# A new order of the work slots in the token mixers of a one-layer hybrid decoder

## The chip, the cores and the metric
The kernel runs on one core of one Trainium2 chip. The metric is the device time of one execution in microseconds, as the median over runs of the same program.

## What is computed
One layer of a decoder runs for a prompt of 256 tokens and for 8 sample tokens with the same weights, all in float32, so 264 columns stand side by side. The layer has token mixers, cross-attention into 256 memory tokens, and a squared-ReLU MLP. The change touches the token mixers alone:

```python
proj = x @ p["w_in"] + p["b_in"]      # columns for four branches and four gates per channel
# A gated DeltaNet: short conv on q, k, v, then the chunked delta rule, 8 heads, gated RMSNorm
out_a = rms_norm(o_a, p["a_norm_w"]) * silu(z_a)
# B Conformer convolution: GLU, depthwise conv of width 31, LayerNorm, swish
u_b, _ = causal_dwconv(a_b * sigmoid(g_b), conv_b, p["b_conv_w"])
out_b = silu(layer_norm(u_b + p["b_conv_b"], p["b_ln_g"], p["b_ln_b"]))
# C short gated convolution, width 3
out_c = bg_c * causal_dwconv(cg_c * h_c, conv_c, p["c_conv_w"])[0]
# D mLSTM matrix memory, 4 heads
y = sum_n(sigmoid(gate_n) * (branch_n @ w_branch_n)) @ p["w_out"]
```

The chunked rules of A and D also update states, which are outputs too.

## The kernel before
**Slots.** All large matrix products are cut into 704 slots. A slot is one weight tile of 128 x 1024 floats: 24 matmuls of 264 columns, since every product is made of three (high x high, high x low, low x high parts of both operands). *slot* (line 207) appends a weight source, a function for TensorE and, at the end of an output block, a *post* function that takes the block out of PSUM. *gin* (line 371) makes one output block of the input projection, two slots. *run* (line 289) walks through the slots. In each it issues the load of a later weight tile, its conversion to the high part on ScalarE (*feed*, line 266) and the split into the low part (*feed_lo*, line 278) two slots ahead. Every fourth split goes to GpSimd, the others to VectorE (line 209).

**Work between the slots.** Two queues of Python generators hold the rest. *chain* has the serial work: the row stage (line 480), the four delta rule units (*a_unit*, line 688, two heads each), the norm of branch B (*b_norm*, line 988) and the two mLSTM units (*d_unit*, line 1071). In each slot *run* issues at most one step of the generator at its head, and then steps of *fill* as long as a planned VectorE time is not ahead of a planned TensorE time:

```python
            if chain and dv_t[0] < lim:
                step(chain)
            while fill and dv_t[0] < lim:
                step(fill)
```

The plan counts 2.72 us a slot (line 303) and a formula for VectorE (line 116). *drain* (line 223) steps a queue until a given generator is through. The instructions are then scheduled once more, by priority in the order of issue (line 1840). TensorE, VectorE, ScalarE, GpSimd and SP each run their queue in order.

**Branch A.** *a_gemm(u)* (line 1264) makes the six blocks of q, k, v for unit u. Each one's post function (*a_block*, line 622) does a convolution of width 4 on VectorE and a sigmoid on ScalarE. The last one appends the unit to *chain*. *a_begin* (line 613) runs at the first block of units 2 and 3 and drains the unit two before it, whose buffer it takes. A unit has a front (norms of q and k: matmuls ssl2q, ssl2k; products KQ and G; masks), five levels of a triangular inverse (matmuls xb, ub, tb), and four chunks (matmuls ks, db, ob, sb) with the states of the sample tokens (DMA dbc, tile s) between them.

**Branch B.** *b_block(j)* (line 955), called a gated block here, makes one of eight blocks: four slots, a gate by exp, ln, exp on ScalarE (*sigmoid*, line 166), and then *b_conv* (line 936), 30 VectorE instructions (tile cB) that go to *fill*. *b_block(j)* drains the convolution two before it. *b_norm* normalises all eight blocks.

**Branch C.** *c_block(j)* (line 897) makes one of eight blocks in six slots, with some six VectorE instructions. The result goes to pairC.

**Output stages.** *phase2(n, pair, first)* (line 1003) makes, for each of 16 output blocks, the gate (two slots, the hardware's sigmoid function on ScalarE) and the branch's product (one slot). The first one is for branch C, in slots 128 to 175.

**The order.** Units 0 and 1 of branch A are first, then B and C blocks in turn, with units 2 and 3 between:

```python
    a_gemm(0)
    a_gemm(1)
    bc((0, 1))
    a_gemm(2)
    bc((2, 3, 4))
    a_gemm(3)
    bc((5, 6, 7))
    phase2(2, "C", True)
```

Of the kernel before, what the change touches and what calls it, by code (L numbers as in the profile page):

```python
# [26 lines left out]
NB = BW // P  # L27
# [64 lines left out]
def decoder_step(ctx, tc, A, O):  # L92
# [12 lines left out]
    def X16(name, dt=F32R):  # L105
        return xp.tile([P, KB, NT], dt, tag="x16", name=name)
# [15 lines left out]
    def act(out, in_, func, bias=0.0, scale=1.0, **kw):  # L122
        return AC.activation(out, in_, func, bias=bias, scale=scale, **kw)  # L123

    def tt(out, a, b, op, eng=None):
        if eng is None:
            cost(out)
        return (eng or DV).tensor_tensor(out=out, in0=a, in1=b, op=op)  # L128

    def ts(out, a, s1, op0, s2=None, op1=None):  # L130
        cost(out, 0.6)
        if op1 is None:
            DV.tensor_scalar(out, a, s1, None, op0=op0)
        else:
            DV.tensor_scalar(out, a, s1, s2, op0=op0, op1=op1)

    def stt(out, a, s, b, op0, op1):
        cost(out, 1.1)
        return DV.scalar_tensor_tensor(out=out, in0=a, scalar=s, in1=b, op0=op0, op1=op1)  # L139
# [14 lines left out]
    def split(hi, lo, src):  # L154
        act(hi, src, AF.Copy)
        tt(lo, src, hi.bitcast(F32), SUB)
# [9 lines left out]
    def sigmoid(g, src, bias=None):  # L166
        if bias is None:
            ts(g, src, -80.0, MAX)
        else:
            ts(g, src, bias, ADD, -80.0, MAX)  # L170
        act(g, g, AF.Exp, scale=-1.0)
        act(g, g, AF.Ln, bias=ones[:, 0:1])
        act(g, g, AF.Exp, scale=-1.0)
# [17 lines left out]
    def col(name, i=0, n=1):  # L191
        o, w = _pc[name]
        return pc[:, o + i:o + i + n]
# [8 lines left out]
    chain, fill = deque(), deque()  # L202
# [12 lines left out]
    def step(q):  # L215
        try:
            next(q[0])
            return True
        except StopIteration:
            q.popleft()  # L220
            return False

    def drain(g):
        for q in (chain, fill):
            while g in q:
                step(q)
# [12 lines left out]
    def later(n, f):  # L239
        todo.append((now[0] + n, f))  # L240

    def store(dst, src):
        later(DELAY, lambda: dma(dst, src))
# [127 lines left out]
    def gin(start, post):  # L371
        i = BI[start]
        gemm(A["win"][i - 1], xs, 2, lambda ps: post(ps, col("bin", i)))
# [221 lines left out]
    def sconv(win, wc, W, dst, eng=None):  # L595
        t = tp.tile([P, NS, W], F32, tag="cw%d" % W, name="cw", bufs=1)
        tt(t[:], win, wc[:, None, :].to_broadcast([P, NS, W]), MUL, eng=GP)
        DV.reduce_sum(out=dst, in_=t[:], axis=AX.X)
        cost(t[:])
# [292 lines left out]
    def newpair(name):  # L892
        return xp.tile([P, 2, NB, NT], F32R, tag="x16", name=name)
# [3 lines left out]
    def c_block(j):  # L897
        st = {}

        def post_h(ps, bc):  # L900
            if j == 0:
                drain(rowg[0])
                pr["C"] = newpair("pairC")
            st["h"] = tp.tile([P, NT], F32, tag="ht", name="ht", bufs=1)
            act(st["h"][:], ps, AF.Identity, bias=bc)

        def post_c(ps, bc):
            e = tp.tile([P, 30 + NT], F32, tag="ext", name="extC", bufs=1)
            GP.memset(e[:, 0:2], 0.0)
            stt(e[:, 2:2 + NT], ps, bc, st["h"][:], ADD, MUL)  # L910
            GP.tensor_copy(winC[:, j, :, 2], e[:, 2 + NP:2 + NT])
            GP.tensor_copy(scp[:, j, :], e[:, NP:NP + 2])
            wc = col("cC", 3 * j, 3)
            v = tp.tile([P, NT], F32, tag="cu", name="cuC", bufs=1)
            act(v[:, 0:NP], e[:, 0:NP], AF.Copy, scale=wc[:, 0:1])
            for i in range(1, 3):
                stt(v[:, 0:NP], e[:, i:i + NP], wc[:, i:i + 1], v[:, 0:NP], MUL, ADD)
            sconv(winC[:, j], wc, 3, v[:, NP:])
            st["v"] = v

        def post_b(ps, bc):
            v = st["v"]
            stt(v[:], ps, bc, v[:], ADD, MUL)
            split(pr["C"][:, 0, j, :], pr["C"][:, 1, j, :], v[:])
            if j == NB - 1:
                store(O["sc_p"], scp[:])
                store(O["sc_s"], winC[:])

        gin(O_H + P * j, post_h)
        gin(O_CG + P * j, post_c)  # L930
        gin(O_BG + P * j, post_b)

    bst = {}
    bgen = {}

    def b_conv(j, e):
        cB = bst["cB"]
        wc = col("cB", 31 * j, 31)
        dst = cB[:, j, :]
        act(dst[:, 0:NP], e[:, 0:NP], AF.Identity, bias=col("bcb", j), scale=wc[:, 0:1])  # L940
        yield
        for i in range(1, 31):
            stt(dst[:, 0:NP], e[:, i:i + NP], wc[:, i:i + 1], dst[:, 0:NP], MUL, ADD)
            if i % 2 == 0:
                yield
        if j == 0:
            bst["m"] = mean0(cB, w1)
        tt(dst, dst, bst["m"][:], SUB, eng=GP)
        bst["ln"].add(j)

    def win_b(j):
        bst["w"] = tp.tile([P, NS, 31], F32, tag="winB", name="winB", bufs=2)
        dma(bst["w"][:], A["sB"][:, j])

    def b_block(j):
        st = {}

        def post_a(ps, bc):
            if j == 0:
                bst["cB"] = w1.tile([P, NB, NT], F32, tag="h8", name="cB", bufs=2)  # L960
                bst["ln"] = Norm(bst["cB"], NB, "B", w1, True)
            st["a"] = tp.tile([P, NT], F32, tag="ht", name="at", bufs=1)
            act(st["a"][:], ps, AF.Identity, bias=bc)

        def post_g(ps, bc):
            if j >= 2:
                drain(bgen[j - 2])
            g = tp.tile([P, NT], F32, tag="sg", name="gB")
            sigmoid(g[:], ps, bc)
            e = tp.tile([P, 30 + NT], F32, tag="extB", name="extB")  # L970
            win = bst["w"]
            if j < NB - 1:
                later(3, lambda: win_b(j + 1))
            GP.memset(e[:, 0:30], 0.0)
            tt(e[:, 30:], st["a"][:], g[:], MUL, eng=GP)
            GP.tensor_copy(win[:, :, 30], e[:, 30 + NP:])
            store(O["gl_p"][:, j], e[:, NP:NP + 30])
            store(O["gl_s"][:, j], win[:])
            dst = bst["cB"][:, j, NP:]
            sconv(win, col("cB", 31 * j, 31), 31, dst)  # L980
            ts(dst, dst, col("bcb", j), ADD)
            bgen[j] = b_conv(j, e)
            fill.append(bgen[j])

        gin(O_GLU + P * j, post_a)
        gin(O_GLU + BW + P * j, post_g)

    def b_norm():
        for j in range(NB):
            drain(bgen[j])  # L990
        ln = bst["ln"]
        yield from ln.finish()
        yield
        for j in range(NB):
            t = ln.block(j, col("blg", j), pool=j % 2)
            sg = tp.tile([P, NT], F32, tag="ht", name="sgB", bufs=1)
            act(sg[:], t, AF.Sigmoid, bias=col("blb", j))
            stt(t, t, col("blb", j), sg[:], ADD, MUL)
            yield

    merged = []

    def phase2(n, pair, first):
        for d in range(KB):
            st = {}

            def post_g(ps, bc, d=d, st=st):
                if first and d == 0:
                    merged.append(X16("merged", F32))
                st["s"] = tp.tile([P, NT], F32, tag="sg", name="gate")  # L1010
                last["SIG"] = act(st["s"][:], ps, AF.Sigmoid, bias=bc)

            def post_p(ps, d=d, st=st):
                sg = st["s"]
                m = merged[0][:, d, :]
                if first:
                    tt(m, ps, sg[:], MUL)
                else:
                    tt(sg[:], ps, sg[:], MUL)
                    tt(m, m, sg[:], ADD, eng=GP)  # L1020
                if n == 3:
                    split(mhl[0][:, d, :], mhl[1][:, d, :], m)

            gin(O_G + D * n + P * d, post_g)
            gemm([A["wbr"][n, d]], lambda: (pr[pair][:, 0], pr[pair][:, 1]), 1, post_p)
# [239 lines left out]
        for i in range(4 if u == 0 else 0, 6):  # L1265
            gin(O_QKV + P * ((i // 2) * 8 + 2 * u + i % 2), a_block(u, i))

    def bc(js):
        for j in js:
            b_block(j)  # L1270
            c_block(j)

    a_gemm(0)
    a_gemm(1)
    bc((0, 1))
    a_gemm(2)
    bc((2, 3, 4))
    a_gemm(3)
    bc((5, 6, 7))
    phase2(2, "C", True)  # L1280
    bng = b_norm()
    mark(lambda: chain.append(bng))
    mark(lambda: [drain(agen[u]) for u in range(4)])
# [569 lines left out]
```

## Time and profile before
| | us |
|---|---|
| median of 3 runs | 2326.68 |
| lowest and highest run | 2324.32, 2328.25 |
| the profiled execution | 2324.7 |
| its span | 2322.9 |
| TensorE busy in the span | 2249.0 (97%) |
| VectorE busy | 1269.8 (55%) |
| ScalarE busy | 1167.0 (50%) |
| GpSimd busy | 977.8 (42%) |

Times in the profile count from the start of the span. PE is TensorE, DVE is VectorE, ACT is ScalarE, POOL is GpSimd, PEld are TensorE's weight loads. Busy shares are over the whole span and mix stages with different limits. A matmul is named by the tile that it writes and the tiles that it reads: g<-xh,wl is one of the 24 of a slot.

### The profile page before, as it was taken

The numbers are of one execution on the slowest core, as the hardware profiler recorded it, in microseconds if no ns is written. First come the engines' busy times: TensorE is split into PE (matmuls) and PEld (weight loads), VectorE is DVE, ScalarE is ACT, GpSimd is POOL, SyncE is SP. The second block draws the span as 40 slices with busy tenths as digits, with TensorE's granted clock in tenths as the row PEclk, the third lists the DMA queues.
The fourth block names the chain that finished last, engine by engine and source line by source line (L and its number), as shares of the span: only waits on it lengthen the run. The fifth ranks groups of instructions, "written<-read, shape, count | busy, mean of one in ns | idle before, by whom it ended". The sixth has DMA issues, their size and how long they took to land.

```text
span 2322.9 us, 46442 instructions
## 1 busy us (share of the span) xinstructions
PE 2249.0 (97%) x19034; PEld 2205.4 (95%) x19034; DVE 1269.8 (55%) x2039; ACT 1167.0 (50%) x1789; POOL 977.8 (42%) x733
## 2 busy tenths in 40 slices
PE   9899999989999999999989999989999999999997
PEld 8899898989999999999989998889999999999997
DVE  7998998894464455433474566385323323323323
ACT  6756456554554455544434555456435435534543
POOL 4535335341222133433243365165445544544576
PEclk9999999999999999999999999999999999999998
DMA  7556455554656676765556666545565565566553
GB/s 233 166 151 201 137 174 167 169 165 143 193 173 185 195 221 215 211 182 182 182 183 182 200 200 201 187 132 181 181 182 176 179 182 181 174 183 181 176 180 127
DMA packets 125134, 418.81 MB, mean 180 GB/s; under 512 B 15608, under 2 KB 20984, under 8 KB 124920
## 3 DMA queue, kind: packets, MB, share of 16 engines
q1 hardware_dynamic: 124920, 415.84, 58.4%
q8 instruction: 149, 2.44, 0.4%
q14 instruction: 65, 0.53, 0.1%
HBM read 401.37 MB, written 14.41 MB: 179 GB/s over the span
## 4 chain that ended last, share of the span: by engine, by line
PE 81%; DVE 13%; issue 3%; DMA 1%; ACT 1%; POOL 1%; DVEq 0%; POOLq 0%; ACTq 0%; SPq 0%
PE g L150 73%; DVE cB L139 3%; DVE wl L128 3%; PE q L150 1%; DVE cu L139 1%; DVE y L128 1%; PE pv L150 1%; DVE y L139 1%; DMA dbc<-dd 1%; PE ub L150 0%; PE xb L150 0%; DVE s L139 0%; PE cb L150 0%; ACT wh L123 0%; PE nb L150 0%
## 5 line engine op out<-in xcount | busy, mean ns | idle before, releaser
L123 ACT ACTIVATE wh<-raw 128x1024 fp32r<-128x1024 f32 (+1 forms) x705 | 745.4, 1058 | 822.4 <-PE g L150 306.3
L128 POOL TENSOR_TENSOR wl<-raw,wh 128x1024 fp32r<-128x1024 f32 x240 | 588.0, 2450 | 724.7 <-PE g L150 483.2
L150 PE MATMUL g<-xh,wl 128*128 128x264 f32 x2496 | 714.0, 286 | 8.1 <-DVE wl L128 6.0
L150 PE MATMUL g<-xl,wh 128*128 128x264 f32 x2496 | 717.2, 287 | 0.0
L150 PE MATMUL g<-xh,wh 128*128 128x264 f32 x2496 | 716.1, 287 | 0.9 <-ACT wh L123 0.9
L128 DVE TENSOR_TENSOR wl<-raw,wh 128x1024 fp32r<-128x1024 f32 (+1 forms) x465 | 589.8, 1269 | 231.2 <-PE g L150 169.6
L150 PEld LDWEIGHTS g<-xh,wl 128*128 128x128 f32 x2496 | 473.0, 190 | 10.2 <-DVE wl L128 6.6
L150 PEld LDWEIGHTS g<-xh,wh 128*128 128x128 f32 x2496 | 473.5, 190 | 5.3 <-issue 2.5
L150 PEld LDWEIGHTS g<-xl,wh 128*128 128x128 f32 x2496 | 472.2, 189 | 2.3 <-issue 1.3
L150 PE MATMUL g<-hgh,wl 128*128 128x264 f32 x1024 | 290.4, 284 | 0.0
L150 PE MATMUL g<-hgl,wh 128*128 128x264 f32 x1024 | 290.4, 284 | 0.0
L150 PE MATMUL g<-hgh,wh 128*128 128x264 f32 x1024 | 289.9, 284 | 0.0
L150 PE MATMUL g<-zh,wh 128*128 128x266 f32 x960 | 275.1, 287 | 0.8 <-DVE zw L128 0.8
L150 PE MATMUL g<-zl,wh 128*128 128x266 f32 x960 | 274.6, 286 | 0.0
L150 PE MATMUL g<-zh,wl 128*128 128x266 f32 x960 | 274.4, 286 | 0.0
L150 PEld LDWEIGHTS g<-hgl,wh 128*128 128x128 f32 x1024 | 193.0, 188 | 0.0
L150 PEld LDWEIGHTS g<-hgh,wh 128*128 128x128 f32 x1024 | 192.5, 188 | 0.0
L150 PEld LDWEIGHTS g<-hgh,wl 128*128 128x128 f32 x1024 | 192.4, 188 | 0.0
L128 DVE TENSOR_TENSOR y<-y,g 128x264 f32<-128x264 f32 x80 | 34.3, 429 | 278.7 <-PE g L150 278.7
L150 PEld LDWEIGHTS g<-zh,wh 128*128 128x128 f32 x960 | 181.4, 189 | 1.0 <-ACT wh L123 1.0
L150 PEld LDWEIGHTS g<-zl,wh 128*128 128x128 f32 x960 | 181.7, 189 | 0.0
L150 PEld LDWEIGHTS g<-zh,wl 128*128 128x128 f32 x960 | 180.8, 188 | 0.0
(481 smaller groups left out, 3449.3 us busy)
## 6 DMA issues: line engine op xcount, KB each, us to landing
raw<-in_win_dram SPq DMA_DIRECT2D x312, 512.0 KB, 4.0
raw<-in_f_dram SPq DMA_DIRECT2D x248, 512.0 KB, 4.2
raw<-in_wbr_dram SPq DMA_DIRECT2D x64, 512.0 KB, 4.0
raw<-in_wout_dram SPq DMA_DIRECT2D x32, 512.0 KB, 4.3
s<-in_sS_dram SPq DMA_DIRECT2D x8, 512.0 KB, 5.0
dbc<-dd SPq DMA_DIRECT2D x16, 256.0 KB, 3.7
out_S_s_dram<-s SPq DMA_DIRECT2D x8, 512.0 KB, 5.2
c<-in_sCm_dram SPq DMA_DIRECT2D x8, 512.0 KB, 5.7
```

The costliest lines, as they stand in the source:

```text
L123: return AC.activation(out, in_, func, bias=bias, scale=scale, **kw)
L128: return (eng or DV).tensor_tensor(out=out, in0=a, in1=b, op=op)
L139: return DV.scalar_tensor_tensor(out=out, in0=a, scalar=s, in1=b, op0=op0, op1=op1)
L150: PE.matmul(out, lhsT, rhs, start=start, stop=stop)
```

## The change
The blocks of branch C come ahead of most of branch B. Only four gated blocks are left before the output stage of branch C. The other four stand inside it, ahead of its output blocks 1, 5, 9 and 12. The projections of units 2 and 3 start 12 and 8 slots later. *b_norm* no longer drains the convolutions: it yields until all eight blocks are made and none is left in *fill*.

```diff
     def b_norm():
-        for j in range(NB):
-            drain(bgen[j])
+        while len(bgen) < NB or any(g in fill for g in bgen.values()):
+            yield
         ln = bst["ln"]
...
-    def phase2(n, pair, first):
+    def phase2(n, pair, first, between={}):
         for d in range(KB):
+            if d in between:
+                b_block(between[d])
             st = {}
...
-    def bc(js):
-        for j in js:
-            b_block(j)
-            c_block(j)
-
     a_gemm(0)
     a_gemm(1)
-    bc((0, 1))
+    c_block(0)
+    b_block(0)
+    c_block(1)
+    c_block(2)
+    c_block(3)
+    b_block(1)
     a_gemm(2)
-    bc((2, 3, 4))
+    c_block(4)
+    b_block(2)
+    c_block(5)
+    c_block(6)
+    b_block(3)
     a_gemm(3)
-    bc((5, 6, 7))
-    phase2(2, "C", True)
+    c_block(7)
+    phase2(2, "C", True, {1: 4, 5: 5, 9: 6, 12: 7})
```

## Rows read from the trace of the kernel before

**Rows 1.** The page's slices: busy tenths of TensorE and VectorE in 40 equal parts

```profile
PE   9899999989999999999989999989999999999997
...
DVE  7998998894464455433474566385323323323323
```

**Rows 2.** The chain that ended last: start us, us, what; a stretch without waits

```profile
972.04 195.07 PE g L150 x1608
```

**Rows 3.** Windows A:B, length; busy us of PE, PEld, DVE, ACT, POOL; clock; DMA

```profile
119.00:187.00 68.00, 65.26 (x659) 63.12 (x654) 63.14 (x122) 32.11 (x58) 17.95 (x22) 1.00 0.50 148
...
240.00:352.00 112.00, 105.33 (x1026) 101.90 (x1026) 107.19 (x198) 50.58 (x88) 38.91 (x43) 0.98 0.53 158
352.00:399.00 47.00, 42.11 (x387) 40.36 (x385) 37.95 (x58) 32.91 (x61) 28.35 (x41) 1.00 0.55 173
399.00:477.00 78.00, 78.00 (x780) 76.19 (x777) 68.99 (x136) 37.68 (x70) 23.48 (x26) 1.00 0.54 166
477.00:516.00 39.00, 32.42 (x251) 30.95 (x250) 37.33 (x58) 23.91 (x35) 18.31 (x14) 0.96 0.53 164
```

**Rows 4.** Windows, as in rows 3: before the output stage, and the output stage

```profile
93.00:516.00 423.00, 399.74 (x3761) 387.11 (x3761) 379.17 (x667) 232.50 (x414) 175.20 (x206) 0.99 0.55 168
516.00:665.00 149.00, 148.20 (x1394) 145.75 (x1394) 67.81 (x107) 69.76 (x102) 30.08 (x17) 1.00 0.56 169
```

**Rows 5.** Waits of TensorE from 93 to 516 us: total us, times, longest

```profile
PE KQ L150 <- DVE qkv L128: 5.3, 2, 3.0
PE ssl2q L150 <- ACT sql2q L123: 4.4, 2, 2.6
PE xb L150 <- DVE m_u L128: 3.1, 2, 1.8
PE ks L150 <- DVE S L139: 2.9, 2, 2.0
PE xb L150 <- DVE m_u L818: 2.8, 3, 1.9
PE db L150 <- DVE vt L139: 2.1, 2, 1.2
```

**Rows 6.** Windows, as in rows 3: two stretches at a low clock

```profile
288.00:291.40 3.40, 3.40 (x17) 3.40 (x17) 3.22 (x10) 3.22 (x9) 0.16 (x1) 0.52 0.00 0
...
513.20:516.60 3.40, 3.40 (x17) 3.40 (x17) 3.40 (x8) 0.18 (x1) 1.03 (x2) 0.51 0.75 258
```

**Rows 7.** VectorE's groups from 93 to 516 us: busy us, mean ns, idle before

```profile
L139 DVE SCALAR_TENSOR_TENSOR cB<-extB,pc,cB 128x256 f32<-128x256 f32 x239 | 145.7, 610 | 8.1 <-ACT cB L123 4.3
L128 DVE TENSOR_TENSOR wl<-raw,wh 128x1024 fp32r<-128x1024 f32 x82 | 107.1, 1307 | 5.9 <-PE g L150 3.6 <-issue 2.0 <-ACT wh L123 0.3
```

**Rows 8.** Tile merged: ns min/median/max, first and last start us

```profile
L128 DVE TENSOR_TENSOR merged<-g,gate x16: 418/433/435, 511.8 to 665.0; 128x264 f32<-128x264 f32 x16
```

**Rows 9.** Windows, as in rows 3: projections of the third and fourth unit

```profile
179.00:222.00 43.00, 40.05 (x327) 39.39 (x326) 34.86 (x66) 25.73 (x48) 21.29 (x35) 1.00 0.66 210
344.00:385.00 41.00, 36.11 (x293) 34.83 (x292) 36.14 (x51) 29.05 (x55) 26.23 (x39) 1.00 0.54 170
```

**Rows 10.** Timeline of ScalarE from 609 us: start us, us, instruction

```profile
609.82 0.46 ACT L123 ACTIVATE gate<-g,pc 128x264 f32<-128x264 f32 x1
610.30 1.28 ACT L123 ACT_TABLE_LOAD   x1
...
612.47 1.28 ACT L123 ACT_TABLE_LOAD   x1
...
614.31 2.11 ACT L123 ACTIVATE wh<-raw 128x1024 fp32r<-128x1024 f32 x2
```

**Rows 11.** Tiles winB, sgB and KQd, columns as in rows 8

```profile
L237 SPq DMA_DIRECT2D winB<-in_sB_dram x8: 425/426/1551, 22.1 to 442.9; - x8
...
L123 ACT ACTIVATE sgB<-cB,pc x8: 499/514/517, 675.2 to 691.4; 128x264 f32<-128x264 f32 x8
...
L150 PE MATMUL KQd<-qkvD x32: 222/222/270, 759.1 to 867.6; 128*64 128x64 f32 x32
```

## The prediction
> **What bounds the kernel now.** I read the page's slices first. TensorE is full in nearly every slice. VectorE is nearly full in the first nine (up to about 520 us) and between 30% and 60% for most of the rest [rows 1]. So the stage that the change reorders has two engines close to their limit, and the rest has one. Where TensorE has nothing to wait for, a slot of 24 matmuls costs 24 x 195.07 / 1608 = 2.91 us [rows 2]. The change neither adds nor removes a matmul, so it can only win or lose time in which TensorE stands, or runs at half clock.
>
> That time I read from stretches of the span [rows 3]. 119 to 187 and 240 to 352 us are long stretches with gated-block convolutions nearly without a break. VectorE is 93% and 96% busy there, and TensorE stands 68 - 65.26 = 2.7 us and 112 - 105.33 = 6.7 us. 352 to 399 us has the end of the fourth unit's projections and the front of the third unit's delta rule, no convolution, VectorE at 81%: TensorE still stands 4.9 us. 399 to 477 us has VectorE at 88% and TensorE loses nothing. 477 to 516 us holds the last convolutions and the front of the fourth unit: VectorE 96%, 6.6 us lost. Over 93 to 516 us that is 423 - 399.74 = 23.3 us, and 516 to 665 us (the output stage of the short convolution) adds 0.8 us [rows 4].
>
> So VectorE's share alone doesn't say where time goes: 88% costs nothing, 93 to 96% does, and a unit's front costs at 81% as well. The waits say why [rows 5]: TensorE takes its queue in order, and a small matmul of the delta rule stands at its head until a result comes from VectorE (KQ, xb, ks) or ScalarE (ssl2q). Two of the longer waits are followed by 3.4 us with about half the clock granted, 1.2 GHz instead of 2.4: 17 matmuls in 3.4 us [rows 6]. At full clock 17 take 17 x 0.1213 = 2.06 us, so each costs 1.3 us, 2.7 us together. What can be won at most is 23.3 + 0.8 + 2.7 = 26.8 us.
>
> **The change, part by part.**
>
> *Four gated blocks go to the output stage.* One block brings 30 convolution steps of 0.610 us mean, 18.3 us of VectorE, four slots, three of whose splits fall to VectorE at 1.31 us [rows 7], and three small steps, put at the 0.43 us of a pass over one output block [rows 8], 1.3 us. The stretch 93 to 516 us has 379 us of VectorE in 423 us, 90% [rows 4]. It loses 4 x 18.3 + 12 x 1.31 + 4 x 1.3 = 94 us and is 16 x 2.91 = 46.6 us shorter: 285 of 376 us, 76%. The output stage goes from 67.8 of 149 us to 67.8 + 94 = 162 of 196 us, 83%. Both lie below the 88% that costs nothing.
> For 240 to 352 us, with half as many convolutions ahead of the output stage, I take three quarters of 6.7 us: -5.0 (bounds 0 and -6.7; nearest is the 88% row, which says all of it, but the unit fronts within the stretch argue for a rest).
> For 477 to 516 us: the fourth unit's front now falls into the output stage, at 83%. The 81% row with a front lost 4.9 us, the 88% row without one none; I take half of 6.6: -3.3 (bounds 0 and -6.6).
>
> *The third unit starts 12 slots later, the fourth 8.* The first block of the third unit empties the first unit's generator (line 615). Before, it does this at slot 45, when the first unit still has steps left, so they are issued in one go; after, at slot 57. A unit has some 36 steps, one is issued a slot, and the row stage ahead of it is through at about slot 19, so by slot 57 the first unit is done. The two ks waits (2.9 us in all [rows 5]) fall in that end, behind state updates on VectorE: -2.9 (bounds 0 and -2.9).
> On the other side, the second and fourth gated blocks now stand directly before those units' projections, so their convolutions run into them. Before, these stretches have 43 - 34.9 = 8.1 us and 41 - 36.1 = 4.9 us of VectorE to spare [rows 9], against 18.3 us each. The projections were issued earlier than most of the convolution and go first; the convolution can spread into the short convolution blocks behind. Price between 0 and the loss of the dense stretch (6.7 / 112 = 6%) over 84 us, +5.0; I take the middle, +2.5.
>
> *Half clock.* The first low stretch follows a wait of the 240 to 352 us part, the second the 3 us KQ wait of the fourth unit: three quarters and a half of 1.3 us, -1.7 (bounds 0 and -2.7).
>
> *ScalarE's tables.* The gate of the output stage uses the sigmoid function, a gated block exp, ln, exp. In the output stage a change between them costs one load of 1.28 us each way, and a second between ln and exp [rows 10]. A gated block brings up to four, 16 in all, 20.5 us of ScalarE. The row's burst of two loads holds ScalarE for 614.31 - 609.82 = 4.5 us before the next weight conversion, and the whole stage around it lost 0.8 us [rows 4]: weights are two slots ahead. A gated block's burst is about 4 x 1.28 + 3 x 0.46 = 6.5 us if no conversion goes between, 2.0 us past what that row covers. Price 0 to 4 x 2.0 = +8; I take 0, since ScalarE has 149 - 69.8 = 79 us free there [rows 4] and conversions can go between.
> The Trainium skill (ScalarE: Activation LUTs, Table sets: the hidden batching unit) says to batch activations by table set, which speaks against mixing the two kinds. It counts one load for ln and then exp and, under What ACT_TABLE_LOAD costs, 2.66 us for a switch with its drain. By that a block has two switches, 8 x 2.66 = 21.3 us in all against my 20.5, an estimate from that page. The trace disagrees on the one load (two around ln) and agrees on its 1.28 us.
>
> *Queues and buffers.* SP issues one weight load a slot as before, and a block's state load and two stores move with it, of which the load takes 0.43 us to issue [rows 11]: nothing changes in what a slot asks of SP but for these, so 0. GpSimd keeps every fourth slot. *b_norm* now polls instead of draining; it starts at the same slot as before. Its last sigmoid came at 691.4 us, and the units queued behind it first reach TensorE at 759.1 us [rows 11]: 68 us of cover, so 0 even if the last convolution is late.
>
> **Sum.** -5.0 - 3.3 - 2.9 - 1.7 + 2.5 = -10.4 us. The profiled execution took 2324.7 us (span 2322.9), 2.0 below the median of 2326.7; from it the sum is 2314.3, and against the median 2316.3. I forecast 2316 us.
>
> **Rivals.**
> *Waits follow latency, not load (no change).* The 352 to 399 us row lost 4.9 us at 81%, so fronts may lose as much anywhere, and the table loads add links to the fourth unit's front. Then only a quarter of the dense stretch and part of ks is won, about 4 us, and the bursts give 2 back: 2325. For it: KQ, ssl2q and the first xb row of the waits are fronts, 12.8 us [rows 5]. Against it: ks, the second xb row and db, 7.8 us, are not. That the written order does not become the order that runs belongs here: the program is scheduled once more by priority (line 1840), and where that keeps the old order of VectorE's work, nothing moves. Chance 0.27.
> *Everything goes (large gain).* VectorE never limits again, fronts included: 2326.7 - 26.8 = 2300. The 88% row is for it, the 81% row against. Chance 0.10.
> *Slower: the convolutions of the second and fourth gated blocks against the third and fourth units' projections.* Excess of VectorE work there is (18.3 - 8.1) + (18.3 - 4.9) = 23.6 us. If the convolution steps are queued on VectorE ahead of the second and third units' fronts, TensorE waits for about half of it, 11.8 us, and only the dense stretch's 5.0 is won: 2326.7 + 6.8 = 2333.5. It decides once VectorE reaches about 96% between the projections. Against it: convolution steps come last in the queue. Chance 0.18.
>
> **How the numbers follow.** Forecast 0.45, large gain 0.10, no change 0.27, slower 0.18. A difference under 0.2% (4.7 us) can't be told from none by the runs. Faster is 0.45 + 0.10 = 0.55. The likeliest case alone spans 2309 to 2322. The range 2303 to 2333 takes in the no-change case and most of the slower one, and leaves out half of each outer case: about 0.15.
>
> **What would show it.** Right: total TensorE standing between 93 us and the output stage's end falls from 24 to about 14 us; VectorE at 75 to 80% before that stage and near 80% in it; no ks wait; 15 to 20 more table loads with no TensorE wait behind them. Wrong: waits on KQ, xb or ssl2q that are longer at the third unit's front, VectorE at 96% in the projections of the third and fourth units, or TensorE waiting for wh behind table loads.

## The result, and the profile after
The changed kernel takes 2340.76 us (median of 4 runs, 2338.44 to 2342.01) against 2327.34 us before: ratio 1.0059, 95% interval 1.0041 to 1.0076. It is slower by 13.4 us, outside the forecast range of 2303 to 2333.

Counting 24 large matmuls a slot, the two traces compare as follows (us; differences are of unrounded times; the spans differ by 15.3):

| slots | before | after | difference |
|---|---|---|---|
| up to 24 | 93.1 | 94.8 | +1.7 |
| 24 to 128 | 402.0 | 394.3 | -7.7 |
| 128 to 192 | 217.2 | 239.6 | +22.4 |
| 192 to the last slot's start | 1589.2 | 1588.0 | -1.1 |

So the part ahead got shorter, and the stretch that took in the gated blocks, with the first norm behind it, grew by three times as much. Not all of that was won and lost. Slots 24 to 128, first in the kernel before, then after (columns as in [rows 3]):

```profile
93.07:495.03 401.96, 381.93 (x3625) 370.16 (x3624) 359.45 (x635) 219.37 (x397) 168.87 (x202) 1.00 0.55 167
```

```profile
94.82:489.08 394.26, 380.86 (x3607) 369.96 (x3606) 305.13 (x543) 215.21 (x378) 150.05 (x180) 0.99 0.55 166
```

TensorE stands 20.0 and 13.4 us there, 6.6 less. But 18 matmuls of the units moved behind slot 128 (3625 to 3607), and the trace has three stretches of 3.4 us at half the clock where there was one (238 to 245 us is two of them, 395 us the third). At some 1.5 us for each, an estimate from the 17 matmuls in [rows 6] and the share granted, the clock takes back 3 of the 6.6 us; the rest of the 7.7, 4 to 5 us, is work that moved.

Windows of the kernel after, first ahead of the output stage, the stage up to slot 128, and slots 128 to 192, then the projections of the third and fourth unit:

```profile
94.00:430.00 336.00, 324.35 (x3124) 314.52 (x3123) 268.46 (x474) 180.67 (x322) 138.78 (x173) 0.98 0.55 167
430.00:489.00 59.00, 57.25 (x492) 56.18 (x490) 37.37 (x70) 35.01 (x58) 12.09 (x9) 1.00 0.52 158
489.00:728.00 239.00, 222.32 (x1929) 216.82 (x1929) 179.18 (x285) 142.44 (x201) 70.52 (x51) 0.97 0.54 164
...
214.00:257.00 43.00, 40.49 (x311) 39.39 (x310) 39.70 (x66) 27.52 (x50) 25.97 (x33) 0.92 0.52 161
370.00:411.00 41.00, 37.19 (x360) 35.53 (x359) 40.78 (x78) 22.87 (x42) 19.89 (x33) 0.96 0.48 157
```

And the window of the kernel before that answers to the third of them, slots 128 to 192:

```profile
495.00:712.00 217.00, 212.97 (x1914) 209.53 (x1913) 126.05 (x192) 113.39 (x163) 49.59 (x29) 0.99 0.57 173
```

Ahead of the output stage VectorE is at 268.5 / 336 = 80%. From 489 to 728 us TensorE stands 16.7 us, against 4.0 us before, while VectorE is at only 75%. The granted clock is 0.97 there against 0.99: four stretches of 3.4 us at half rate against one, some 5 us more lost. The last 5 us of the 22.4 are the work that moved here. ScalarE has 142 us of work against 113. TensorE's waits in the kernel after, from 430 to 728 us (total us, times, longest):

```profile
PE KQ L150 <- DVE qkv L128: 4.2, 1, 4.2
PE g L150 <- DVE wl L128: 3.7, 3, 2.4
PE ssl2k L150 <- ACT sql2k L123: 3.2, 1, 3.2
PE db L150 <- DVE vt L139: 3.1, 3, 2.5
PE ks L150 <- DVE S L139: 1.9, 2, 1.2
PE g L150 <- POOL wl L128: 1.1, 1, 1.1
PE xb L150 <- DVE m_u L818: 0.9, 1, 0.9
```

The rows on wl are new in kind: large matmuls wait for their weights, which [rows 5] did not have. They make 4.8 of 18.1 us. The other 13.3 us stand in front of the units' own small matmuls, whose inputs come through passes on ScalarE and VectorE. ScalarE's groups, first after (430 to 728 us), then before (430 to 712 us); columns as in [rows 7]:

```profile
L123 ACT ACTIVATE wh<-raw 128x1024 fp32r<-128x1024 f32 x80 | 84.2, 1056 | 89.9 <-PE g L150 40.3 <-DMA raw<-in_win_dram 35.2 <-DMA raw<-in_wbr_dram 11.4
L123 ACT ACT_TABLE_LOAD x29 | 37.2, 1283 | 0.5
```

```profile
L123 ACT ACTIVATE wh<-raw 128x1024 fp32r<-128x1024 f32 x82 | 86.5, 1058 | 102.2 <-PE g L150 62.0 <-DMA raw<-in_win_dram 28.2 <-DMA raw<-in_wbr_dram 10.4
L123 ACT ACT_TABLE_LOAD x10 | 12.8, 1283 | 0.2
```

There are 29 table loads where there were 10. A weight conversion that waits for PE is ahead of need, since it waits for a free buffer; one that waits for a DMA is not ahead. The first kind fell from 62 to 40 us, the second rose from 39 to 47. So the feed lost some of its lead; e12_one_table below shows that this alone costs little. One gated block's burst, its gate passes with the loads between them, on ScalarE's timeline of the kernel after:

```profile
586.00 1.06 ACT L123 ACTIVATE wh<-raw 128x1024 fp32r<-128x1024 f32 x1 [0.64 <-PE g L150]
587.08 1.28 ACT L123 ACT_TABLE_LOAD   x1
588.37 0.42 ACT L123 ACTIVATE gB<-gB 128x264 f32<-128x264 f32 x1
588.70 0.36 ACT L123 ACTIVATE dl<-db 64x256 f32<-64x256 f32 x1
589.08 1.28 ACT L123 ACT_TABLE_LOAD   x1
590.38 0.52 ACT L123 ACTIVATE gB<-gB,ones 128x264 f32<-128x264 f32 x1
590.91 1.28 ACT L123 ACT_TABLE_LOAD   x1
592.20 0.42 ACT L123 ACTIVATE gB<-gB 128x264 f32<-128x264 f32 x1
592.53 1.04 ACT L123 ACTIVATE wh<-raw 128x1024 fp32r<-128x1024 f32 x1
...
595.57 1.28 ACT L123 ACT_TABLE_LOAD   x1
```

From 587.08 to 592.53 us, 5.5 us, ScalarE converts no weights; three loads, the gate's three passes and one pass of the unit (dl) stand in that time, and the fourth load follows at the next gate.

### The profile page after: what moved, and what is told of

It reads as the page before. It is cut to its first block, busy times and chain, and to the rows that moved or that the text cites. A ratio compares the mean times of both kernels' runs of the same rounds, so it can differ in the third digit from the quotient of the medians.

```text
span 2338.2 us, 46470 instructions
## 1 busy us (share of the span) xinstructions
PE 2258.0 (97%) x19034; PEld 2213.7 (95%) x19034; DVE 1268.8 (54%) x2039; ACT 1191.7 (51%) x1808; POOL 979.5 (42%) x733
## 4 chain that ended last, share of the span: by engine, by line
PE 76%; DVE 15%; issue 4%; ACT 3%; DMA 2%; POOL 1%; DVEq 0%; SPq 0%; POOLq 0%; ACTq 0%
PE g L150 69%; DVE cB L139 4%; DVE wl L128 3%; DVE cu L139 2%; DVE y L128 1%; PE q L150 1%; PE pv L150 1%; ACT wh L123 1%; DVE y L139 1%; DMA raw<-in_win_dram 1%; ACT L123 1%; DMA raw<-in_xq_dram 0%; PE xb L150 0%; PE ub L150 0%; PE cb L150 0%
## 5 line engine op out<-in xcount | busy, mean ns | idle before, releaser
L150 PE MATMUL g<-xh,wl 128*128 128x264 f32 x2496 | 717.5, 287 | 13.4 <-DVE wl L128 9.7
```

The costliest lines, as they stand in the source:

```text
L150: PE.matmul(out, lhsT, rhs, start=start, stop=stop)
```

## The experiments
The kernel before ran beside each group of runs on the same chip, at 2326.6 to 2327.5 us. Ratios are to it, with their 95% intervals.

**Table or VectorE: four runs.** The first takes the loads away from the gated blocks:

```diff
-            sigmoid(g[:], ps, bc)
+            if j < 4:
+                sigmoid(g[:], ps, bc)
+            else:
+                act(g[:], ps, AF.Sigmoid, bias=bc)
```

> The changed kernel, with the gate of the four gated blocks inside the output stage made by the sigmoid function (one ScalarE pass) in place of exp, ln, exp. Table theory (the 19 more table loads of the changed kernel, 35 against 16, hold up ScalarE and with it the delta rule unit and the weight conversions): loads fall to about 20, the TensorE idle time from 489 to 728 us falls by about half, time near 2329 us, at least 8 us below the changed kernel's 2341. VectorE theory (the convolutions inside the output stage stand ahead of the unit's work on VectorE): loads fall but the waits stay, 2338 to 2341 us.

Measured: 2325.12 us, 0.9993 (0.9984 to 1.0003), with 21 loads. The loss is gone: 15.6 us below the changed kernel, where the table theory said some 12. Eight ScalarE and four VectorE passes went with the loads; e12_one_table below keeps them.

The second takes the sigmoid function out of the stage instead:

```diff
+                if first:
+                    sigmoid(st["s"][:], ps, bc)
+                    return
                 last["SIG"] = act(st["s"][:], ps, AF.Sigmoid, bias=bc)
```

> The changed kernel, with the 16 gates of the first output stage made by exp, ln, exp, as the gated blocks' gates are, in place of the sigmoid function: no table load at all until that stage ends, at the price of 16 more VectorE passes of 0.49 us and 32 more ScalarE passes of 0.45 us. Table theory: 4 to 6 loads less than with any other order, the long waits on ssl2k and KQ of the fourth unit shrink to under 2 us, time near 2325 us. VectorE theory: 8 us more VectorE work in a stage that it limits, 2342 to 2346 us.

Measured: 2326.01 us, 1.0000 (0.9990 to 1.0009), no load from 430 us to the norm of branch B. More work on both engines, and 14.7 us less than the changed kernel.

The third was to add loads to the kernel before:

```diff
+    dmy = cp.tile([P, 1], F32, name="dmy")
...
+                if first and d in (1, 5, 9, 12):
+                    for f in (AF.Exp, AF.Ln, AF.Exp):
+                        act(dmy[:], dmy[:], f)
```

> The kernel before, with three ScalarE passes over one column (exp, ln, exp, on a tile that nothing else reads) ahead of gates 1, 5, 9 and 12 of the output stage: about 16 more table loads at four places and nothing else. Table theory: if holding ScalarE is enough, 4 to 10 us over the kernel before, with waits of TensorE on wh, wl or the unit's results behind the loads. VectorE theory: within 2 us of the kernel before.

Measured: 2326.22 us, 0.9997 (0.9988 to 1.0007). It tells nothing, as the tile's rows in its trace show (columns as in [rows 8]): with nothing to wait for, the twelve passes were scheduled at 2 to 10 us, long before the stage, where no load was needed.

```profile
L123 ACT ACTIVATE dmy<-dmy x12: 184/195/206, 2.0 to 10.1; 128x1 f32<-128x1 f32 x12
```

The fourth takes VectorE work away and leaves the loads:

```diff
-        for i in range(1, 31):
+        for i in range(1, 31 if j < 4 else 3):
```

> The changed kernel, with 2 in place of 30 VectorE instructions in the convolutions of the four gated blocks inside the output stage (28 of 31 taps of those blocks are left out). VectorE theory: about 50 us of VectorE work less in the output stage and its waits go, 2325 us or less. Table theory: the loads stay, the waits behind them stay, 2335 to 2340 us.

Measured: 2333.17 us, 1.0025 (1.0016 to 1.0034), 35 loads: between the two ranges. The waits on ssl2k and KQ stay (4.0 and 3.2 us), but 7.6 us of the time go: VectorE has a share in the loss.

**Placed loads, and the parts of the change alone.** The third run again, tied to its place by its input:

```diff
+    dmy = cp.tile([P, 1], F32, name="dmy")
...
+                if first and d in (1, 5, 9, 12):
+                    act(dmy[:], ps[:, 0:1], AF.Exp)
+                    act(dmy[:], dmy[:], AF.Ln, bias=ones[:, 0:1])
+                    act(dmy[:], dmy[:], AF.Exp)
```

> The kernel before, with three ScalarE passes over one column (exp, ln, exp) ahead of gates 1, 5, 9 and 12 of the output stage, the first of them reading that gate's own product, so that they run at those four places: about 16 more table loads, no more VectorE work, no convolution moved. If holding ScalarE is what costs: 8 us or more over the kernel before. If the loads cost only where results wait behind them (the fourth unit's norms, the gated block's own convolution): 0 to 4 us over the kernel before.

Measured: 2330.83 us, 1.0017 (1.0008 to 1.0027), 31 loads against 16. Fifteen loads, with twelve passes over one column, cost 4.2 us in the kernel before with nothing else moved. That is half of what was expected if holding ScalarE is what costs, and just above the range for loads that cost only where results wait behind them.

The order ahead of the stage alone:

```diff
     c_block(7)
-    phase2(2, "C", True, {1: 4, 5: 5, 9: 6, 12: 7})
+    for j in range(4, 8):
+        b_block(j)
+    phase2(2, "C", True)
```

> The changed kernel's order up to the output stage, but with the last four gated blocks in one row directly ahead of that stage and none inside it. Load theory (what the first part gained, 8 us by slot 128, comes from convolutions that were moved out of it): the gain is gone and the four convolutions meet the fourth unit's front, 2328 to 2335 us. Order theory (it comes from the later third and fourth units and the short convolution blocks ahead): 2317 to 2322 us.

Measured: 2330.01 us, 1.0015 (1.0005 to 1.0024). That is 3.4 us slower than the kernel before, in the range of the load theory. It doesn't part the order from the table loads, though: this run has 24 of them against 16, since the later norms of the third and fourth unit fall between the stage's sigmoid gates.

The move into the stage alone (several calls are put on one line here, and the lines of the new order that they replace are left out):

```diff
+    b_block(0); c_block(0); b_block(1); c_block(1)
+    a_gemm(2)
+    b_block(2); c_block(2); b_block(3); c_block(3); c_block(4)
+    a_gemm(3)
+    c_block(5); c_block(6)
     c_block(7)
     phase2(2, "C", True, {1: 4, 5: 5, 9: 6, 12: 7})
```

> Gated blocks 4 to 7 inside the output stage as in the changed kernel, gates by exp, ln, exp there as well, but the first four gated blocks, the short convolution blocks and the projections of the third and fourth unit in the order of the kernel before (gated and short in turn). Table theory: the loads are as many, the stage loses as much, 2335 to 2342 us whatever the order ahead. Delay theory (the fourth unit's front was pushed into the stage by the later projections): 2325 us or less.

Measured: 2341.02 us (4 runs), 1.0055 (1.0040 to 1.0071), 36 loads. The loss does not depend on the order ahead of the stage.

The sigmoid function (the first run's edit), and the blocks earlier in the stage:

```diff
-    phase2(2, "C", True, {1: 4, 5: 5, 9: 6, 12: 7})
+    phase2(2, "C", True, {0: 4, 4: 5, 7: 6, 10: 7})
```

> The changed kernel with the sigmoid function in the four gated blocks inside the stage, and these at output blocks 0, 4, 7 and 10 in place of 1, 5, 9 and 12, so that the last convolution ends before the norm of branch B starts. If the wait of 2.7 us on wl at the start of that norm, and the low clock after it, come from the late convolution: 2319 to 2322 us, 3 to 5 us under the run with the sigmoid function alone. If not: 2325 us or more.

Measured: 2322.67 us, 0.9985 (0.9975 to 0.9994): 2.4 us below the sigmoid function alone, a little less than expected and near the edge of what these runs can tell apart. In the trace the wait of a large matmul at the start of branch B's norm (2.6 us in e1_sigmoid_gate) is gone.

**What is left without loads.** Sigmoid function and short convolutions together (edits of the first and fourth run):

> The run with the sigmoid function in the four gated blocks inside the stage, and their convolutions cut from 30 to 2 VectorE instructions (28 of 31 taps of those blocks are left out): neither the loads nor the VectorE work. The convolution with loads cost 7.6 us (the changed kernel against the run with the short convolutions alone). If load and convolution each cost by themselves: 2317 to 2319 us. If the convolution costs only behind the loads, because it is set free late and in one piece by a late gate: 2322 to 2326 us.

Measured: 2321.81 us, 0.9977 (0.9967 to 0.9986). The convolutions cost 2325.1 - 2321.8 = 3.3 us without the loads and 2340.8 - 2333.2 = 7.6 us with them; the loads cost 11.4 us without the convolutions and 15.6 us with them. The time lies between the two expected ranges, nearer to the second: the convolutions cost a little by themselves, and more beside the loads.

Exp, ln, exp for all gates of the stage (the second run), with the blocks at 0, 4, 7 and 10:

> The run with exp, ln, exp for all 16 gates of the first output stage (no load in it), with the gated blocks at output blocks 0, 4, 7 and 10. If the 3.8 us wait at the norm of branch B and the low clock behind it came from the late last convolution: 2320 to 2323 us. If the additional passes on VectorE and ScalarE limit: 2326 us or more.

Measured: 2317.62 us (4 runs, 2315.84 to 2318.22), 0.9961 (0.9946 to 0.9976): faster than both kernels and than its expected range, and 8.4 us below the second run. Its window from slot 128 to 192, and behind it the same window of e12_one_table (below):

```profile
489.00:705.00 216.00, 214.31 (x1935) 210.97 (x1935) 170.26 (x291) 122.12 (x202) 68.12 (x47) 1.00 0.60 182
```

```profile
487.00:711.00 224.00, 217.14 (x1938) 212.98 (x1937) 179.63 (x285) 130.06 (x192) 68.98 (x51) 0.99 0.57 175
```

In the first, TensorE stands 1.7 us, at full clock throughout, with VectorE at 79%. Two things changed against the second run: the last convolution ends earlier, and so do the norm's exp and ln passes, which now come ahead of the first sigmoid gates of branch A's output. There is one load in this window where the second run has five. The run can't say which of the two is worth how much.

The old order ahead, with the edits of e8_sigmoid_earlier:

> The old order ahead of the stage (gated and short blocks in turn, third unit not delayed) with the sigmoid function in the four gated blocks inside the stage, at output blocks 0, 4, 7 and 10. If the new order ahead of the stage is worth what the first part of the changed kernel's trace shows (6 to 8 us by slot 128): 2328 to 2331 us. If it is worth nothing: 2321 to 2325 us.

Measured: 2323.57 us, 0.9980 (0.9971 to 0.9990), against 2322.67 with the new order. The order ahead is worth 1 us at most, which these runs can't tell from nothing.

The same passes with fewer loads:

```diff
-            sigmoid(g[:], ps, bc)
+            if j < 4:
+                sigmoid(g[:], ps, bc)
+            else:
+                ts(g[:], ps, bc, ADD, -80.0, MAX)
+                last["TAB"] = after(AC.preload_act_table_set("natural_log_exp_and_others"), "SIG")
+                last["SIG"] = after(act(g[:], g[:], AF.Exp, scale=-1.0), "TAB")
+                act(g[:], g[:], AF.Ln, bias=ones[:, 0:1])
+                act(g[:], g[:], AF.Exp, scale=-1.0)
```

> The changed kernel with an explicit load of the table set that holds both exp and ln ahead of each gated block's gate inside the stage: two loads a block in place of up to four, so about 8 loads less (27 against 35), all passes as in the changed kernel. Table theory: about half of the 15.6 us that the sigmoid function saved, 2331 to 2336 us. If only leaving exp and ln altogether helps (the three passes in a row are the delay, not the loads): 2338 to 2341 us.

Measured: 2323.89 us, 0.9988 (0.9978 to 0.9997), 16.9 us below the changed kernel. Its groups, from 430 to 711 us, have 18 loads where the changed kernel has 29, and one block's gate follows without any (columns as in [rows 7] and [rows 10]):

```profile
L123 ACT ACTIVATE wh<-raw 128x1024 fp32r<-128x1024 f32 x80 | 84.3, 1057 | 92.1 <-DMA raw<-in_win_dram 36.6 <-PE g L150 32.8 <-DMA raw<-in_wbr_dram 11.4
L123 ACT ACT_TABLE_LOAD x14 | 18.0, 1283 | 0.2
...
L973 ACT ACT_TABLE_LOAD x4 | 5.1, 1283 | 0.1
```

```profile
512.48 0.41 ACT L123 ACTIVATE gB<-gB 128x264 f32<-128x264 f32 x1
512.92 0.52 ACT L123 ACTIVATE gB<-gB,ones 128x264 f32<-128x264 f32 x1
513.34 1.05 ACT L123 ACTIVATE wh<-raw 128x1024 fp32r<-128x1024 f32 x1
514.30 0.40 ACT L123 ACTIVATE gB<-gB 128x264 f32<-128x264 f32 x1
```

This is the cleanest of the runs: the same passes on the same engines in the same slots, 11 loads less, 14.1 us less on ScalarE, and the whole loss is gone, where about half was expected. Not only the number of loads changed: each explicit load is tied behind an earlier gate of the stage, so it stands well ahead of its block (at 496.19 us for the gate shown), and the fourth unit's first norm, between the two, finds the table already loaded. TensorE's waits from 430 to 728 us:

```profile
PE g L150 <- DVE wl L128: 2.7, 2, 2.2
PE KQ L150 <- DVE qkv L128: 1.4, 1, 1.4
PE ks L150 <- DVE S L139: 1.0, 1, 1.0
PE xb L150 <- DVE m_u L818: 0.9, 1, 0.9
PE xb L150 <- DVE m_u L128: 0.6, 1, 0.6
PE db L150 <- DVE vt L139: 0.2, 1, 0.2
```

Against the changed kernel, the waits in front of the units' matmuls fall from 13.3 to 4.1 us and those for weights from 4.8 to 2.7. One stretch at half the clock is left of four in slots 128 to 192, which is worth some 4.5 us. Together that is about 16 of the 16.9 us. So by these two traces most of the loss came as waits for results of the units, and the smaller part as waits for weights. The conversions' lead is no better here than in the changed kernel: they wait 32.8 us for a free buffer and 48.0 for DMAs, against 40.3 and 46.6.

**Where the loads hurt.** Gated block 5 away from the fourth unit's front:

```diff
-    phase2(2, "C", True, {1: 4, 5: 5, 9: 6, 12: 7})
+    phase2(2, "C", True, {1: 4, 8: 5, 10: 6, 12: 7})
```

> The changed kernel with gated block 5 at output block 8 and block 6 at 10 in place of 5 and 9, so that no gated block's gate meets the fourth unit's norms (slots 134 to 142); gates by exp, ln, exp as in the changed kernel, loads about as many. If the loads cost where they meet the front (two waits of 3.2 and 4.2 us and the low clock behind each): 2330 to 2334 us. If they cost wherever they stand: 2338 to 2343 us.

Measured: 2340.05 us (4 runs), 1.0053 (1.0036 to 1.0070), 38 loads. The gated block's meeting with the front is not the cause. The front's KQ wait is gone, but ssl2k still waits 3.3 us, with two loads of the unit's own norm (515.21 and 517.38 us) ahead of it on ScalarE. The last block's burst in this run holds weights back for 7.2 us, from the start of the first load (635.51) to two conversions in a row (642.71):

```profile
635.51 1.28 ACT L123 ACT_TABLE_LOAD   x1
...
637.25 1.28 ACT L123 ACT_TABLE_LOAD   x1
...
639.38 1.28 ACT L123 ACT_TABLE_LOAD   x1
...
642.71 1.99 ACT L123 ACTIVATE wh<-raw 128x1024 fp32r<-128x1024 f32 x2
...
652.90 1.06 ACT L123 ACTIVATE wh<-raw 128x1024 fp32r<-128x1024 f32 x1 [4.24 <-DMA raw<-in_win_dram]
```

A late conversion frees its raw buffer late, so the next weight load starts late: none is issued from 636.14 to 649.09 us, and that one lands at 652.81. The price comes when TensorE has used up the lead: it waits for wl 1.3 us at 647.05 and 2.5 us at 658.30. The wait for a DMA is not itself a price: behind the burst of [rows 10] a conversion waits for one for 4.6 us too (at 621.05), and TensorE waits for nothing.

Exp, ln, exp for the stage's gates in the kernel before (the second run's edit there):

> The kernel before with exp, ln, exp for the 16 gates of the first output stage, nothing moved: the 7 loads that this stage has before go, 16 VectorE passes and 32 ScalarE passes come. If the 2318 us of the run with these gates and the gated blocks moved earlier owe more to the moved blocks: 2324 to 2328 us. If they owe it to the loads that were there before already: 2318 to 2321 us.

Measured: 2325.83 us, 0.9993 (0.9984 to 1.0002): with 7 loads in place of 16, and the additional passes, no gain that is clear of noise. So the best version owes its gain, 8.2 us between these two runs, to the moved blocks, once the loads no longer stand against them.

A fourth buffer for raw weights would test the lost lead by itself; there is no such run.

## Why the prediction was wrong
**The step that failed** is the term for ScalarE's tables: 0 taken, +8 as its upper bound, 15.6 us measured (e1_sigmoid_gate), 16.9 with every pass kept (e12_one_table). The count was near: 16 loads taken, 19 more found (35 against 16), of which the sigmoid function in the gated blocks removes 14. Three readings were not.

First, [rows 10] was taken as proof of cover: one burst of 4.5 us with TensorE full behind it. That burst came after three conversions that had waited for a free buffer, with the lead whole. A burst 100 us earlier in the same trace was not read, in the middle of the fourth unit's norm:

```profile
504.97 1.28 ACT L123 ACT_TABLE_LOAD   x1
506.27 0.48 ACT L123 ACTIVATE gate<-g,pc 128x264 f32<-128x264 f32 x1
506.77 1.28 ACT L123 ACT_TABLE_LOAD   x1
508.06 0.69 ACT L123 ACTIVATE rl2k<-ssl2k,eps 128x512 f32<-128x512 f32 x1
...
508.93 1.28 ACT L123 ACT_TABLE_LOAD   x1
...
510.55 0.63 ACT L123 ACTIVATE rl2k<-rl2k 128x528 f32<-128x528 f32 x1
```

VectorE stands idle for ScalarE for 1.1 us ahead of its pass on that result (qkv, at 511.21 us), and the KQ wait of 3.0 us in [rows 5] stands behind that pass. The prediction put this wait down to VectorE. With no load there (e14_before_exp_ln) it is 1.9 us.

Second, the price was taken from weight conversions alone, as what a burst holds beyond the lead. The waits that went with the loads in e12_one_table are mostly those of the units' matmuls: 9.2 us of them, and 2.1 us of waits for weights.

Third, "conversions can go between" held once, in the second block (at 522.27 us). In the other three blocks none goes between the first load and the last pass; these bursts keep ScalarE from converting for 5.6, 5.5 and 7.5 us. ScalarE's free time, 79 of 149 us, does not say when it is free.

The sign to look for had been named: TensorE did wait for weights behind table loads.

**The rule** that was weighed, to batch passes by table set (the Trainium skill, ScalarE: Activation LUTs, Table sets: the hidden batching unit), pointed the right way and was set aside on the strength of one row. The trace agrees with it: with the passes kept and 11 loads fewer, e12_one_table won 16.9 us. The dispute about one load or two for ln and exp is settled by e12_one_table: once the set with both is loaded, exp, ln and exp follow with no load between (512.48 to 514.30 us); left to themselves, they get one each after a sigmoid pass (587.08 to 590.91 us in the kernel after). The Trainium skill says this on the same page under Rules for kernel authors, where it names that set for exp and ln together. The 2.66 us that the Trainium skill counts there for a switch with its drain (What ACT_TABLE_LOAD costs) do not show: passes start 1.3 us after a load does, in the timelines of both kernels (587.08 to 588.37 us).

**The dense stretches** (-5.0) **and the ks term** (-2.9) held up in the trace in part: TensorE's standing ahead of slot 128 fell by 6.6 us, VectorE's share ahead of the stage came to 80% where 76% was worked out, and no ks wait is left before 430 us. But ks waits of 1.9 us stand behind 430 us instead, and e11_old_order_sigmoid shows that the whole time hardly depends on that order. So the -2.9 was for the most part a wait moved, not a time won.

**Half clock** (-1.7) went the other way. From slot 24 to 192 the kernel before has two low stretches of 3.4 us, the kernel after seven, three of them ahead of slot 128. At some 1.5 us each that is about +7.5. The step tied the low stretches to two waits that were to shrink, and had no price for new ones behind new waits.

**The fourth unit's front** (-3.3) failed: its two waits are 3.2 and 4.2 us instead of 2.6 and 3.0. With the sigmoid function in the gated blocks one long wait of the front stays: ssl2k 2.6 us in e1_sigmoid_gate and 5.3 in e9_sigmoid_short_conv, KQ 4.1 in e8_sigmoid_earlier. With no load in the stage (e2_exp_ln_gates, e10_exp_ln_earlier) both are 0.2 us at most, and with one table (e12_one_table) KQ waits 1.4. This fits that the unit's own norms, which now stand between sigmoid gates, cost loads as well; these were not in the sum.

**The projections** (+2.5) were of about the right size. VectorE is at 92% and 99% there. TensorE stands 2.5 and 3.8 us, not more than before (2.9 and 4.9 us in [rows 9]), but at a clock of 0.92 and 0.96 where both had 1.00, which is worth 4 to 5 us. The rival on the slow side put its loss here; it had the right sign and half the size by another mechanism, and its point of decision, 96%, was passed at the fourth unit without more standing.

**Polling in *b_norm*** was put at 0 even with a late last convolution. That was too little: with the blocks earlier, 2.4 us (e8_sigmoid_earlier) and 8.4 us (e10_exp_ln_earlier) are won. The norm of all eight blocks and the first gates of branch A's output come at once behind the last convolution; how much of this is VectorE's work and how much the four loads that go in e10_exp_ln_earlier is not shown.

**What was right** shows only without the loads: e10_exp_ln_earlier is 8.2 us below e14_before_exp_ln, whose stage has the same gates. The sum forecast 10.4. It took the blocks' earlier places too, so it is no proof of the sum: in the places of the change (e2_exp_ln_gates) nothing is won.

**Open:** 15 loads placed in the kernel before cost 4.2 us, 14 taken from the changed one gave 15.6. The convolutions account for 4 us of that difference, the order ahead for none (e7_between_alone), and the gated block at the front for none (e13_away_from_front). Whether the rest is owed to the units' loads nearby, or to results that wait behind the real passes and not behind the placed ones, is not settled.

## What to carry to other kernels
An engine at 50% can still stop another one that waits for its results: look at the longest stretch in which it is held, and at all that is queued behind it there, the serial work as well as the feed, and not at its free time. When work moves into another stage, list the state that it needs on each engine (here the loaded table) beside its busy time. One covered instance in a trace bounds that instance, not four of them with other work behind each; look for the instances that were not covered, too.

## What had not been expected of the hardware
Removing 11 loads of 1.28 us, 14.1 us of an engine that is not the bottleneck, gave 16.9 us (e12_one_table): more than their own length, though four of the loads that are left also stand at other places. Part of it is the clock: the changed kernel has a mean granted clock of 0.97 from 489 to 728 us, the run with one table 0.99, and the run with no load 1.00. Each of the four low stretches in that window of the changed kernel begins in or just behind a wait of TensorE of 2.4 to 4.2 us. So such a wait can cost over a microsecond more than it lasts, as in [rows 6]. Not every one does: behind the 2.6 us on ssl2q in [rows 5] the kernel before shows no low stretch.
